# A planner's table of engine times set to other numbers, in a fused four-branch block

## The chip, the core and the metric

The kernel runs on one core of one Trainium2 chip. The metric is the device time of one execution in microseconds (us), as the median over several runs. The core has a matrix engine (TensorE, "PE" in the profile, with "PEld" for its weight loads), a vector engine (VectorE, "DVE"), a scalar engine (ScalarE, "ACT"), GpSimd ("POOL") and SyncE ("SP"). In this kernel SP issues the loads of the weights, POOL most of the branches' own loads and stores, ACT some stores. Each engine works through its own instructions in the order in which they stand in the program.

## The reference

The kernel computes one layer for 256 tokens of 2048 features in float32. Cut to what matters:

```
h = rmsnorm(x, norm_pre)
q, f, i, z_a, u, z_b, rkvwa, z_c, xbc, dt, z_d, gate_pre = h @ w_in   # 2048 x 21648
o_a = hgrn2(q, f, i) * silu(z_a)       # gated linear attention, chunks of 64
o_b = s5(u, ...) * silu(z_b)           # diagonal complex state space model, GLU
o_c = rwkv7(rkvwa, ...) * silu(z_c)    # delta rule, 16 heads of 64
o_d = mamba2(xbc, dt, z_d)             # SSD, 16 heads of 64
merged = sum_b sigmoid(gate_pre[b] + gate_bias[b]) * (o_b @ w_up[b])
out = x + rmsnorm(merged @ w_out, norm_post)
```

## The kernel before

All weights are used once, so the program is one long stream of 444 weight chunks. Each chunk (512 KB) is loaded on SP into `raw` (three buffers), split on ACT into `hi` (a copy in the reduced float32r format, L207) and on DVE into `lo = raw - hi` (L216), and multiplied on PE in three products with a likewise split left side: `pg<-h,hi` twice and `pg<-h,lo` once (L261). `hi` and `lo` have four buffers, so the split of chunk n + 3 is written into the program beside the products of chunk n. In the first part of the stream a chunk is 24 products of 256 columns, later 12 of 512 columns. `pg` is the accumulator of the stream (two buffers in PSUM), `pb` the bank that branch products and transposes use (four banks). `ev` and `evm` are evacuations of `pg`, with a token shift or a convolution.

The branches are generators. Each `yield` ends a stage, a small group of instructions on any engines. The stages are put in between the chunks by `_Stream.run_jobs`: after each chunk it goes through the jobs in order of priority and emits a stage, as long as neither DVE nor ACT is more than `AHEAD` = 3.7 us ahead of PE, where a stage may run only if the job's time stamp lies at most `SLACK` = 1.0 us after PE. These times are no measured times: they are a running estimate, `K.t_pe`, `K.t_dve`, `K.t_act` and so on. Every helper that emits an instruction (`mm`, `tr`, `act`, `tt`, `stt`, `ts`, `ld`, ...) first books its cost with `book` (or `book_dma` for a transfer: 2.0 us and the bytes at 220 KB per us). The estimate is only used to choose the place of each stage in each engine's instruction list.

The branches' names that come up below are these.

- S5 (branch b): its output matrices are loaded (`cn`), masked (`cx`), transposed (`pb<-ident,cx`), evacuated as `cT` and `cng`, and stored; the imaginary part goes through the same tiles after the real one. It then runs in eight tiles of two halves each: loads `us`, `bs`, `cu` on POOL (1.3 MB a tile), products `pb<-us,bs`, four scans into `tb` on DVE, products of `ta` and `tb` with `cu`, and `cu` updated on DVE (two instructions).
- Mamba-2 (branch d): loads `mx`, `mbc`, `dk` on POOL, in two halves; `mrow` holds rows of its step sizes, transposed by `pb<-ident,mrow`.
- RWKV-7 (branch c): sigmoids `sw`, `ic` and squares `sq` on ACT, head sums `pb<-sq,ind`, a store `dinv<-row` and its broadcast load `bc`, scans `cs`, row products `bc`, `k`, Gram blocks `GB` and `L` with masks by POOL's selects, an inverse by back substitution in `XT`, whose result goes through DRAM (`dtt`, `dtn`) into `T` and `TT`, and products `pb<-T,GB`.

Of the kernel before, what the change touches and what calls it, by code (L numbers as in the profile page):

```python
# [60 lines left out]
PE_GAP = 0.0  # L61
# [5 lines left out]
# the functions that each activation table serves  # L67
# [6 lines left out]
class _Kern:  # L74
    """Pools, constants and instruction helpers shared by the weight stream and the branches."""

    def __init__(self, ctx, tc, drams):
# [20 lines left out]
        self.soft = False  # L98
        self.o = {}
# [12 lines left out]
    @staticmethod  # L112
    def live(tiles):
        """How many of the tiles are still referred to; the others are dropped from the list."""
        for i in range(len(tiles) - 1, -1, -1):
            if sys.getrefcount(tiles[i]) <= 2:
                del tiles[i]
        return len(tiles)
# [4 lines left out]
    def wait(self, n):  # L123
        """Until n more slots are free."""
# [5 lines left out]
    def wait_banks(self, n):  # L130
        """Until n more PSUM banks are free."""
# [5 lines left out]
    def fm(self, name, n=2):  # L137
        """A feature-major [128, 4 n, 256] array, in tiles of four feature tiles."""
        return [self.big([128, 4, 256], name=f"{name}{j}") for j in range(n)]
# [22 lines left out]
    def book(self, engine, cost, out, ins):  # L162
        """Book an instruction: it starts when the engine is free and its operands are there."""
# [31 lines left out]
    def act(self, out, in_, func, **kw):  # L195
# [7 lines left out]
        ins = [in_] + [x for x in (kw.get("scale"), kw.get("bias")) if hasattr(x, "tensor")]  # L203
        self.book("t_act", cost, out, ins)
# [4 lines left out]
    def _dve(self, out, ins, ns):  # L209
        """Book a vector instruction; one that reads the last one's output waits for it."""  # L210
        self.book("t_dve", 0.06 + ns * 1e-3, out, ins)
# [15 lines left out]
    def stt(self, out, in0, scalar, in1, op0, op1, **kw):  # L227
        self._dve(out, (in0, in1), self._n(out) * 1.045)
        return self.nc.vector.scalar_tensor_tensor(out=out, in0=in0, scalar=scalar, in1=in1, op0=op0, op1=op1, **kw)  # L229

    def ts(self, out, in0, s1, s2, op0, op1=None):
        self._dve(out, (in0,), self._n(out) * 0.53)
# [21 lines left out]
    def mm(self, out, lhsT, rhs, start=True, stop=True, **kw):  # L254
        n = self._n(rhs)
        if rhs.dtype == F32R:
            cost = n * 0.427e-3 if n >= 256 else n * 1.67e-3
        else:
            cost = max(n * 1.67e-3 * min(out.shape[0], 128) / 128, 0.027)
        self.book("t_pe", cost + PE_GAP * (1 if rhs.dtype == F32R else 2), out, (lhsT, rhs))  # L260
        return self.nc.tensor.matmul(out, lhsT, rhs, start=start, stop=stop, **kw)  # L261

    def tr(self, out, in_, b=0):
        """out = in_ transposed; in_ starts at partition b."""
# [12 lines left out]
    def ld(self, out, in_):  # L277
        """A transfer whose source may still be under way."""
# [3 lines left out]
    def ldx(self, out, in_):  # L282
        """A load of what has long been in DRAM."""
# [5 lines left out]
    def st(self, out, in_):  # L289
        """A store of what the scalar engine has just written."""  # L290
# [11 lines left out]
    def split(self, hi, lo, src):  # L302
        """src (float32 in SBUF) as the exact sum of two float32r parts."""
# [3 lines left out]
    def rstd(self, out, ss, n, eps):  # L307
        """out = 1 / sqrt(ss / n + eps), small tiles."""
# [5 lines left out]
def setup_consts(K):  # L314
    nc = K.nc
    d = K.d
# [22 lines left out]
    # ind[:, g, :] sums each half of the partitions into rows 2 g and 2 g + 1 of 32  # L339
# [15 lines left out]
    # lmask[s, level, t]: s and t (mod 64) are paired at that level of the binary split; level 0 is the diagonal  # L355
# [26 lines left out]
def head_sum(K, ps, i, sq):  # L382
    """Sums over each head's features of tile i, to rows 32 (i % 4) + 2 (i // 4) + half of ps."""
# [4 lines left out]
def bcast_heads(K, dst, src):  # L388
    """src DRAM [4, 4, 256] to dst (two tiles [128, 4, 256]): row (q, 2 g + e) on the 64 partitions of half e."""
# [5 lines left out]
# ---------------------------------------------------------------- RWKV-7  # L395
def rwkv_branch(K, rw):
    """rw: r, k, v (two tiles [128, 4, 256]) and wda [128, 256], after the token shift. Leaves K.o['c']."""
# [94 lines left out]
    # L1[c][e]: on the 64 key partitions of head parity e, rows (a | r) scaled by the decay;  # L492
    # on the other 64 partitions the masked products of k with them
# [37 lines left out]
    for c in range(4):  # L531
# [34 lines left out]
        # token-major copies of the scaled keys  # L566
# [261 lines left out]
def hgrn_half(K, g, load):  # L828
# [42 lines left out]
    k = f  # L871
# [1417 lines left out]
```

## Time and profile before

| what | value |
|---|---|
| median of 3 runs | 1427.38 us (1424.73 to 1429.43) |
| profiled execution, its span | 1427.8 us |
| PE busy | 1390.9 us, 97% |
| DVE busy | 1038.0 us, 73% |
| ACT busy | 827.1 us, 58% |
| POOL busy | 162.0 us, 11% |
| bytes moved | 288.62 MB, mean 202 GB/s |
| chain that ended last | PE 71%, DMA 8%, DVE 8%, issue 6%, ACT 6% |

A time in the profile counts from the start of the span. In a row of the chain stand the start, the duration and the work; in a row of a timeline also, in brackets, the idle time of the engine before it and what ended it. A row of a window shows, for each engine, its busy time and the number of instructions in that window, and at the end the granted clock of TensorE (1.00 is full), the share of the DMA engines that was busy, and GB/s. Buffer numbers are left out of the names there; the lists of instructions below keep them, so `hi43_1895` is the `hi` of chunk 43.

### The profile page before, as it was taken

Reading aid. Unit: us, or ns where it says so; the run is one execution under the profiler, and the core shown is the slowest. Engines: PE = TensorE matmul, PEld = TensorE weight load, DVE = VectorE, ACT = ScalarE, POOL = GpSimd, SP = SyncE. Lnnn points to the kernel's source line nnn. Section 1 sums busy time; section 2 is a strip of 40 time slices with the busy share of each in tenths; the row PEclk is TensorE's granted clock in tenths of the full one; section 3 lists DMA queues with packets and bytes.
Section 4 is the critical chain, followed back from the end, with each engine's and each line's share of the span. In section 5 each row is a group of like instructions: output and inputs, shape, how many; then the busy total and the mean of one; then the engine's idle time right before and its main releaser. Section 6 shows DMA issues by size and latency. Waiting matters only on the chain.

```text
span 1427.8 us, 24645 instructions
## 1 busy us (share of the span) xinstructions
PE 1390.9 (97%) x9751; PEld 1223.2 (86%) x9751; DVE 1038.0 (73%) x1422; ACT 827.1 (58%) x1136; POOL 162.0 (11%) x268
## 2 busy tenths in 40 slices
PE   8999989989999999999999999999999999999997
PEld 7999989989989887888789888888789987888886
DVE  6787488778786784576787699767978788576655
ACT  5455445845456546765578765787556444544442
POOL 6232310010025320011100001000010000000000
PEclk9999999999999999999999999999999999999999
DMA  7878985487657876477876567655686856676664
GB/s 214 239 240 263 279 270 163 135 191 232 206 155 175 228 236 179 142 203 201 232 207 198 181 207 197 211 177 172 193 197 194 214 177 191 213 267 194 183 195 135
DMA packets 199040, 288.62 MB, mean 202 GB/s; under 512 B 12453, under 2 KB 116750, under 8 KB 198926
## 3 DMA queue, kind: packets, MB, share of 16 engines
q1 hardware_dynamic: 169614, 237.15, 54.2%
q0 software_dynamic: 25216, 43.05, 13.9%
q10 hardware_dynamic: 4096, 6.86, 1.4%
q8 instruction: 76, 1.25, 0.3%
q14 instruction: 38, 0.31, 0.1%
HBM read 268.33 MB, written 18.66 MB: 201 GB/s over the span
## 4 chain that ended last, share of the span: by engine, by line
PE 71%; DMA 8%; DVE 8%; issue 6%; ACT 6%; POOL 0%; SPq 0%; ACTq 0%; DVEq 0%; POOLq 0%
PE pg L261 63%; PE pb L261 6%; DMA raw<-in_w_in_dram 6%; DVE lo L216 4%; ACT hi L207 2%; PE pb L267 1%; DVE ta L216 1%; ACT L207 1%; DMA cn<-in_s_c_im_dram 1%; DMA x<-in_x_dram 1%; DVE invtmp L216 0%; ACT hT L207 0%; DVE tb L243 0%; DVE tb L216 0%; DMA ds5b<-bl 0%
## 5 line engine op out<-in xcount | busy, mean ns | idle before, releaser
L216 DVE TENSOR_TENSOR lo<-raw,hi 128x1024 fp32r<-128x1024 f32 x444 | 541.1, 1223 | 350.6 <-ACT hi L207 342.3
L207 ACT ACTIVATE hi<-raw 128x1024 fp32r<-128x1024 f32 x444 | 465.9, 1055 | 532.7 <-PE pg L261 249.1
L261 PE MATMUL pg<-h,hi 128*128 128x256 f32 x2624 | 480.8, 286 | 4.1 <-DVE ev L229 3.6
L261 PE MATMUL pg<-hi,h 128*128 128x512 f32 x1408 | 448.1, 393 | 0.1
L261 PEld LDWEIGHTS pg<-h,hi 128*128 128x128 f32 x2624 | 409.9, 192 | 10.7 <-issue 6.9
L261 PE MATMUL pg<-h,lo 128*128 128x256 f32 x1312 | 371.6, 285 | 5.0 <-DVE lo L216 4.1
L261 PEld LDWEIGHTS pg<-hi,h 128*128 128x128 f32 x1408 | 264.9, 188 | 58.5 <-issue 2.5
L261 PE MATMUL pg<-lo,h 128*128 128x512 f32 x704 | 275.5, 391 | 2.6 <-DVE lo L216 2.4
L261 PEld LDWEIGHTS pg<-h,lo 128*128 128x128 f32 x1312 | 251.0, 192 | 6.7 <-DVE lo L216 5.4
L261 PE MATMUL pg<-hi,o 128*128 128x512 f32 x512 | 164.2, 394 | 0.0
L261 PEld LDWEIGHTS pg<-lo,h 128*128 128x128 f32 x704 | 132.6, 188 | 30.5 <-DVE lo L216 4.5
L261 PEld LDWEIGHTS pg<-hi,o 128*128 128x128 f32 x512 | 96.1, 188 | 21.9 <-issue 1.6
L261 PE MATMUL pg<-lo,o 128*128 128x512 f32 x256 | 99.8, 390 | 0.0
L261 PE MATMUL pg<-hi,mhl 128*128 128x512 f32 x224 | 71.1, 391 | 0.0
L280 POOL DMA_DIRECT2D gb<-in_gate_bias_dram x16 | 8.7, 545 | 541.1 <-DVE gate L216 477.9
L207 ACT ACT_TABLE_LOAD x51 | 65.4, 1283 | 5.3 <-DVE mss L235 2.8
L261 PEld LDWEIGHTS pg<-lo,o 128*128 128x128 f32 x256 | 48.1, 188 | 9.5
L261 PEld LDWEIGHTS pg<-hi,mhl 128*128 128x128 f32 x224 | 42.1, 188 | 8.7
L261 PE MATMUL pg<-lo,mhl 128*128 128x512 f32 x112 | 43.6, 389 | 0.0
L243 DVE TENSOR_TENSOR_SCAN tb<-s5p,ta 128x256 f32<-128x256 f32 x64 | 41.7, 701 | 0.1
L261 PEld LDWEIGHTS pg<-lo,mhl 128*128 128x128 f32 x112 | 21.0, 188 | 4.2
L261 PE MATMUL pg<-ghl,hi 128*128 128x256 f32 x128 | 23.1, 283 | 0.0
(371 smaller groups left out, 1362.6 us busy)
## 6 DMA issues: line engine op xcount, KB each, us to landing
raw<-in_w_in_dram SPq DMA_DIRECT2D x340, 512.0 KB
raw<-in_w_up_dram SPq DMA_DIRECT2D x64, 512.0 KB
raw<-in_w_out_dram SPq DMA_DIRECT2D x32, 512.0 KB
us<-duhl POOLq DMA_DIRECT2D x16, 256.0 KB, 6.4
bs<-ds5b POOLq DMA_DIRECT2D x16, 256.0 KB, 7.6
gb<-in_gate_bias_dram POOLq DMA_DIRECT2D x16, 256.0 KB, 4.7
raw<-in_s_w_glu_dram SPq DMA_DIRECT2D x8, 512.0 KB
x<-in_x_dram SPq DMA_DIRECT2D x4, 512.0 KB
```

The lines of the kernel that those rows point to most:

```text
L207: return self.nc.scalar.activation(out=out, in_=in_, func=func, **kw)
L216: return self.nc.vector.tensor_tensor(out=out, in0=in0, in1=in1, op=op)
L243: return self.nc.vector.tensor_tensor_scan(out=out, data0=data0, data1=data1, initial=0.0, op0=ALU.mult, op1=ALU.add)
L261: return self.nc.tensor.matmul(out, lhsT, rhs, start=start, stop=stop, **kw)
L267: return self.nc.tensor.transpose(out, in_, self.ident[b:b + p, b:b + p])
L280: return self.nc.gpsimd.dma_start(out=out, in_=in_)
```

## The change

The costs that the helpers book are set to other numbers. `PE_GAP` (it was 0) goes. A float32r matmul with 256 columns or more is booked with `n * 0.417e-3 + 0.0133` us in place of `n * 0.427e-3`, and 0.15 us are added whenever matmuls change between the full 128 by 128 array and a part of it. On ACT, 0.09 us are added for each scale or bias that is read from a tile, on DVE 0.065 us for each such scalar of `stt` and `ts`. The other lines of the diff drop comments and docstrings, so that line numbers of the changed kernel are 3 to 9 higher.

```diff
-PE_GAP = 0.0
+POINTER_ACT = 0.09
+POINTER_DVE = 0.065
...
         self.last = None
         self.soft = False
+        self.parted = False
...
         ins = [in_] + [x for x in (kw.get("scale"), kw.get("bias")) if hasattr(x, "tensor")]
+        cost += POINTER_ACT * (len(ins) - 1)
         self.book("t_act", cost, out, ins)
...
-    def _dve(self, out, ins, ns):
-        self.book("t_dve", 0.06 + ns * 1e-3, out, ins)
+    def _dve(self, out, ins, ns, scalars=()):
+        ptr = sum(hasattr(x, "tensor") for x in scalars)
+        self.book("t_dve", 0.06 + ns * 1e-3 + POINTER_DVE * ptr, out, ins)
...
     def stt(self, out, in0, scalar, in1, op0, op1, **kw):
-        self._dve(out, (in0, in1), self._n(out) * 1.045)
+        self._dve(out, (in0, in1), self._n(out) * 1.045, (scalar,))
...
     def ts(self, out, in0, s1, s2, op0, op1=None):
-        self._dve(out, (in0,), self._n(out) * 0.53)
+        self._dve(out, (in0,), self._n(out) * 0.53, (s1, s2))
...
     def mm(self, out, lhsT, rhs, start=True, stop=True, **kw):
         n = self._n(rhs)
         if rhs.dtype == F32R:
-            cost = n * 0.427e-3 if n >= 256 else n * 1.67e-3
+            cost = n * 0.417e-3 + 0.0133 if n >= 256 else n * 1.67e-3
         else:
             cost = max(n * 1.67e-3 * min(out.shape[0], 128) / 128, 0.027)
-        self.book("t_pe", cost + PE_GAP * (1 if rhs.dtype == F32R else 2), out, (lhsT, rhs))
+        parted = out.shape[0] < 128 or lhsT.shape[0] < 128
+        if parted != self.parted:
+            self.parted = parted
+            cost += 0.15
+        self.book("t_pe", cost, out, (lhsT, rhs))
```

The instructions of PE, DVE, POOL and SP stay the same in number; ACT gets four more loads of its function tables (66 in place of 62), because functions of different tables now alternate more often. Some 1800 of PE's 8736 instructions stand elsewhere relative to the others. Three places follow.

The first is ACT where S5's output matrices are evacuated. Before, the transposes stand on PE after the products of chunk 39, and the second ones, for the imaginary part, after chunk 44:

```order
L207 ACTIVATE hi42_1854<-raw42_1786 128x1024
L207 ACTIVATE hi43_1895<-raw43_1818 128x1024
L207 ACTIVATE ev_80_1845<-ev_80_1845 128x512
L292 DMA dbc_96<-ev_80_1845 128x512
L207 ACTIVATE cT_81_1884<-pb_82_1885 128x512
L207 ACTIVATE cT_81_1884<-pb_83_1890 128x512
L207 ACTIVATE cng_84_1930<-pb_82_1885 128x512
L207 ACTIVATE cng_84_1930<-pb_83_1890 128x512
```

In the changed kernel the first transposes stand after chunk 35 and the second ones after chunk 39:

```order
L210 ACTIVATE hi38_1711<-raw38_1645 128x1024
L210 ACT_TABLE_LOAD
L210 ACTIVATE mrow_61_1151<-mrow_61_1151 16x128 x2
L210 ACTIVATE hi39_1754<-raw39_1675 128x1024
L210 ACT_TABLE_LOAD
L210 ACTIVATE ev_76_1702<-ev_76_1702 128x512
L301 DMA dx_95<-ev_76_1702 128x512
L210 ACTIVATE cT_77_1743<-pb_78_1744 128x512
L210 ACTIVATE cT_77_1743<-pb_79_1749 128x512
L210 ACTIVATE cng_82_1797<-pb_78_1744 128x512
L210 ACTIVATE cng_82_1797<-pb_79_1749 128x512
```

Mamba's `mrow` and two table loads stand between the split of chunk 38 and `cT` now, and four chunks lie between the two sets of transposes instead of five.

The second place is POOL's list of loads around Mamba's second half and S5's tile 1. Before:

```order
L280 DMA mx_138_2968<-dx_95 128x1024
L280 DMA mbc_139_2969<-dbc_96 128x512 x2
L280 DMA dk0_143_3010<-dacs_1482 128x8x128
L280 DMA dk1_144_3012<-dacs_1482 128x8x128
L280 DMA lw_157_3258<-in_rwkv_w2_dram 64x1024
L280 DMA lw_157_3258<-in_rwkv_a2_dram 64x1024
L280 DMA bc0_185_3631<-dinv_3626 64x4x256 x2
L280 DMA bc1_186_3632<-dinv_3626 64x4x256 x2
L280 DMA us_188_3708<-duhl_101 64x4x256
L280 DMA bs_189_3709<-ds5b_973 64x8x128
```

In the changed kernel:

```order
L289 DMA mx_141_2960<-dx_95 128x1024
L289 DMA mbc_142_2961<-dbc_96 128x512 x2
L289 DMA us_143_2967<-duhl_101 64x4x256
L289 DMA bs_144_2968<-ds5b_938 64x8x128
L289 DMA us_143_2967<-duhl_101 64x4x256
L289 DMA bs_144_2968<-ds5b_938 64x8x128
L289 DMA cu_145_2973<-ds5c_1215 128x384
L289 DMA cu_145_2973<-du_100 128x256
L289 DMA dk0_147_3007<-dacs_1637 128x8x128
L289 DMA dk1_148_3009<-dacs_1637 128x8x128
L289 DMA lw_159_3136<-in_rwkv_w2_dram 64x1024
L289 DMA lw_159_3136<-in_rwkv_a2_dram 64x1024
```

The six loads of S5's tile 1 (`us`, `bs` twice each, `cu` twice) have moved from behind `bc` to between `mbc` and `dk`.

The third place is DVE ahead of the first products with `T`. Before, these stand on PE after the products of chunk 157:

```order
L216 TENSOR_TENSOR lo157_6213<-raw157_6178,hi157_6212 128x1024
L216 TENSOR_TENSOR lo158_6231<-raw158_6197,hi158_6230 128x1024
L216 TENSOR_TENSOR lo159_6258<-raw159_6216,hi159_6257 128x1024
L229 SCALAR_TENSOR_TENSOR cu_272_5519<-cu_272_5519,pt_115,pb_298_6248 64x256
L216 TENSOR_TENSOR cu_272_5519<-cu_272_5519,pb_298_6248 64x256
L216 TENSOR_TENSOR lo160_6281<-raw160_6234,hi160_6280 128x1024
```

In the changed kernel they stand after chunk 152, so that the splits of 152 to 155 are the last ones ahead of them:

```order
L609 COPY invtmp_293_5683<-XT_292_5682 128x1024
L220 TENSOR_TENSOR lo148_6096<-raw148_6033,hi148_6095 128x1024
L233 SCALAR_TENSOR_TENSOR cu_252_5129<-cu_252_5129,pt_115,pb_298_5784 64x256
L220 TENSOR_TENSOR cu_252_5129<-cu_252_5129,pb_298_5784 64x256
L220 TENSOR_TENSOR lo149_6116<-raw149_6059,hi149_6115 128x1024
L220 TENSOR_TENSOR lo150_6134<-raw150_6099,hi150_6133 128x1024
L220 TENSOR_TENSOR lo151_6163<-raw151_6119,hi151_6162 128x1024
L220 TENSOR_TENSOR lo152_6185<-raw152_6137,hi152_6184 128x1024
L220 TENSOR_TENSOR lo153_6203<-raw153_6166,hi153_6202 128x1024
L220 TENSOR_TENSOR lo154_6221<-raw154_6188,hi154_6220 128x1024
L220 TENSOR_TENSOR lo155_6239<-raw155_6206,hi155_6238 128x1024
```

Before, the update of `cu` stands directly behind the split of chunk 159, at the products with `T`; now it stands behind the split of chunk 148, seven splits ahead of the last one shown.

## The prediction

> **What bounds the kernel now.** I read the page first, then the waits of TensorE, then windows of 50 us, then the chain of waits around each gap.
>
> ```profile
> span 1427.8 us, 24645 instructions
> ...
> PE 1390.9 (97%) x9751; PEld 1223.2 (86%) x9751; DVE 1038.0 (73%) x1422; ACT 827.1 (58%) x1136; POOL 162.0 (11%) x268
> ...
> L216 DVE TENSOR_TENSOR lo<-raw,hi 128x1024 fp32r<-128x1024 f32 x444 | 541.1, 1223 | 350.6 <-ACT hi L207 342.3
> ...
> L207 ACT ACT_TABLE_LOAD x51 | 65.4, 1283 | 5.3 <-DVE mss L235 2.8
> ```
>
> TensorE is busy in 97% of the span, and idle 1427.8 − 1390.9 = 36.9 us, head and tail included. No instruction is dropped, so nothing can be won outside that idle time and the slow clock behind it. The profiled execution (1427.8 us) lies at the median of the runs (1427.38), so the sum is made against 1427.4. The windows show where TensorE loses time (PE busy first, then clock, DMA share, GB/s at the end):
>
> ```profile
> 150.00:200.00 50.00, 44.32 (x346) 43.98 (x345) 31.20 (x48) 21.41 (x29) 11.80 (x18) 0.93 1.08 294
> 400.00:450.00 50.00, 46.98 (x429) 42.26 (x429) 37.53 (x40) 33.41 (x50) 16.64 (x14) 0.97 0.50 143
> 750.00:800.00 50.00, 50.00 (x347) 45.88 (x347) 34.23 (x42) 42.06 (x51) 0.00 (x0) 1.00 0.59 187
> ```
>
> From 750 us on a window is full. What this change can win lies in the first half, where four branches run beside the stream. The waits of TensorE name them (us in total, times, longest):
>
> ```profile
> PE pg L261 <- DVE lo L216: 6.5, 8, 2.2
> ...
> PE pg L261 <- DVE ev L229: 3.6, 1, 3.6
> PE pb L261 <- DVE cu L216: 2.7, 1, 2.7
> PE pb L261 <- DVE tb L216: 2.6, 2, 2.4
> ...
> PE pb L267 <- DVE cx L235: 2.1, 1, 2.1
> ```
>
> The five longest gaps end at 157.4 (cx), 184.2 (ev), 314.4 (lo), 419.7 (tb) and 542.6 us (cu). Each costs more than itself, since the granted clock (third number from the right) is halved behind it:
>
> ```profile
> 157.20:160.70 3.50, 3.34 (x16) 3.37 (x17) 2.47 (x3) 2.56 (x5) 0.00 (x0) 0.51 0.58 166
> 180.00:184.50 4.50, 0.88 (x7) 0.70 (x7) 3.96 (x9) 2.66 (x5) 0.00 (x0) 1.00 1.02 315
> 184.50:188.00 3.50, 3.50 (x19) 3.50 (x18) 1.83 (x3) 3.10 (x6) 0.00 (x0) 0.51 1.03 360
> 188.00:191.50 3.50, 3.50 (x31) 3.50 (x31) 3.38 (x7) 0.32 (x2) 0.00 (x0) 1.00 1.03 340
> 314.20:317.70 3.50, 3.25 (x15) 3.25 (x16) 3.50 (x4) 1.18 (x2) 0.00 (x0) 0.51 1.01 315
> 420.00:423.50 3.50, 3.50 (x22) 2.54 (x15) 2.73 (x4) 0.00 (x0) 0.00 (x0) 0.51 0.86 265
> 542.90:546.40 3.50, 3.50 (x61) 2.95 (x54) 2.32 (x2) 1.06 (x1) 1.04 (x2) 0.51 0.82 241
> ```
>
> After each gap of 2.1 us or more stand some 3.5 us at 0.51 of the clock, then 1.00 again: half of 3.5 us is lost, 1.7 us per gap. The Trainium skill ("TensorE: Matmul & The Clock Gate", section HAM oscillation) warns only of idle gaps above about 3.4 us. By that rule just the 3.6-us gap would bring a slow stretch, and the three other gaps that I take as gone would each be worth 1.7 us less, 5 us in all. This trace does not agree: gaps of 2.1, 2.2, 2.4 and 2.7 us were followed by the half clock too, and the measurement decides.
>
> **What the change does.** It sets only estimates. The chain of waits holds the paces that they should match, with the pieces that the next steps need:
>
> ```profile
> 147.79 8.52 DMA cn<-in_s_c_im_dram
> ...
> 168.57 10.76 DMA raw<-in_w_in_dram
> ...
> 199.43 17.26 PE pg L261 x144
> ...
> 310.41 2.85 DVE bc L229 x7
> ...
> 530.16 9.03 DMA raw<-in_w_in_dram
> ...
> 824.34 16.35 PE pg L261 x72
> ```
>
> 256-wide products take 17.26 / 144 = 0.120 us and 512-wide ones 16.35 / 72 = 0.227 us. Before, the estimate had 0.109 and 0.219; now it has 0.120 and 0.227. A chunk of 24 256-wide products grows in the estimate from 2.62 to 2.88 us. The planner so believes TensorE to be later, and the tests (engines not over 3.7 us ahead of TensorE, a stage's stamp not over 1.0 us ahead) let branch stages in earlier. The dearer pointer operands pull the other way on ACT and DVE, but less. In the order S5 comes forward most: 5 chunks early at its first tile, some 40 at the second half of tile 1, and 12 to 16 later on. So the change moves gaps; I cost the five and what is put in their place.
>
> Gap 1, cx (a loss). S5's output matrices are transposed, evacuated as cT and cng, and only then is the imaginary part cn loaded, masked to cx and transposed again.
>
> ```profile
> 142.57 1.06 ACT L207 ACTIVATE hi<-raw 128x1024 fp32r<-128x1024 f32 x1 [1.20 <-DMA raw<-in_w_in_dram]
> 143.53 0.61 ACT L207 ACTIVATE ev<-ev 128x512 f32<-128x512 f32 x1
> ...
> 144.55 1.09 ACT L207 ACTIVATE cT<-pb 128x512 f32<-128x512 f32 x2 [0.40 <-ACT ev L207]
> 145.52 1.09 ACT L207 ACTIVATE cng<-pb 128x512 f32<-128x512 f32 x2
> ...
> 156.33 0.88 DVE L235 TENSOR_SCALAR cx<-cn,s5pm 128x512 f32<-128x512 f32 x2 [2.92 <-DMA cn<-in_s_c_im_dram]
> ...
> L207 ACT ACTIVATE mrow<-mrow x4: 292/408/419, 93.3 to 122.0; 16x256 f32<-16x256 f32 x2, 16x128 f32<-16x128 f32 x2
> ```
>
> Before, five chunks (14.4 us) stood between the two sets of transposes and TensorE still waited 2.1 us. Now there are four, 2.9 us less cover. Ahead of cT on ACT stand now two table loads (2 × 1.28) and two mrow exponentials (2 × up to 0.41): 3.4 us more, of which 1.6 may fall into the idle 1.20 + 0.40 of these rows. The wait becomes 2.1 + 2.9 + 1.8 to 3.4 = 6.8 to 8.4 us, less about 1 for the six mrow transposes that now stand there; I take 7. The half clock behind it is paid already. Loss 5 us; bounds 3 and 7.
>
> Gaps 2 and 3, transfers that crowd the weight stream:
>
> ```profile
> 162.60 0.66 POOL L280 DMA_DIRECT2D us<-duhl  x1
> ...
> 169.76 0.56 POOL L280 DMA_DIRECT2D mx<-dx  x1
> ...
> 295.36 2.50 POOL L280 DMA_DIRECT2D bc<-dinv  x4 [76.27 <-DMA dinv<-row]
> 297.84 0.64 POOL L280 DMA_DIRECT2D us<-duhl  x1
> ```
>
> Before, S5's loads (us, bs, cu, 1.3 MB) go out right ahead of Mamba's mx and the loads behind it, one weight chunk takes 10.76 us, and ev stands behind the late lo. S5's tile 0 now comes five chunks (14 us) earlier, but the loads of tile 1 fall in with Mamba's second half on the same queue, ahead of its dk. I take 3.0 back of 3.6 + 1.7 = 5.3; bounds 0 and 5.3. In gap 3 the bc loads (1 MB) and S5's tile 1 went out back to back, and now bc stands alone: of 2.2 + 1.7 = 3.9 I take 3.4, bounds 1 and 3.9. What is late next is bc itself, now four chunks behind its store.
>
> Gap 4, tb. POOL's selects ran beside S5's scans:
>
> ```profile
> 410.50 1.47 POOL L275 TENSOR_SCALAR_AFFINE_SELECT GB<-GB 64x1024 f32<-64x1024 f32 x1 [54.77 <-ACT GB L207]
> ...
> 409.75 4.25 DVE L243 TENSOR_TENSOR_SCAN tb<-s5p,ta 128x256 f32<-128x256 f32 x4
> ```
>
> Four scans took 4.25 us there and tb came late. This half stands now in chunk 83, far from the selects; another S5 half is near them. Of 2.4 + 1.7 = 4.1 I take 3.4, bounds 0 and 4.1. Gap 5, cu: the vector engine's cu stood behind a lo whose chunk took 9.03 us, and the products with T waited for its bank. Now no cu stands among the last seven lo ahead of the products with T. 2.7 + 1.7 = 4.4 back; bounds 2 and 4.4.
>
> New places. At chunk 82 ACT must pass eight sigmoids and the squares before TensorE sums them:
>
> ```profile
> 276.43 3.39 ACT L207 ACTIVATE sq<-k,pt 128x256 f32<-128x256 f32 x8
> ...
> L243 DVE TENSOR_TENSOR_SCAN cs<-m,sw 128x512 f32<-128x512 bf16 x4 | 4.6, 1204 | 0.0
> ```
>
> Squares 3.4, sigmoids about 3, hi 1.1 in one split, against two chunks (5.8 us): a wait of 0 to 4, I take 2.5. On the vector engine split 83 gets the four cs scans (4.8 us) with r1 and lo on top of S5's halves. Summing the durations of the trace in the new order, its backlog is 8.7 us there and 5 to 7 at splits 86, 90, 96 and 99 (before: never over 5.0). The lead of lo is three chunks, 8.6 us, so it just covers; I take 1.5 for this and other new tight places, bounds 0 and 20 (below). The four table loads that the new order adds (4 × 1.28 = 5.1 us) lie on ACT, busy 58%, and cost nothing beyond the two counted above; exposed they would cost 5.
>
> Sum: gains 3.0 + 3.4 + 3.4 + 4.4 = 14.2, losses 5.0 + 2.5 + 1.5 = 9.0, net −5.2: 1427.4 − 5.2 = **1422 us**.
>
> **Rivals.** (1) Nothing measurable, 1427 (1423.1 to 1431.7). The gaps only change place: the old order had the same planner and five bad places in 540 us, and a new one has as many. Gains 14 against losses 14. For it: the transfers' estimate is untouched, and two of my losses are of its kind. Against: from 750 us on TensorE never waits, so only half of the stream can go wrong. That the estimates move nothing is excluded by the order. (2) Slower, by one mechanism: the vector engine's backlog from chunk 73 to 100. It decides from the point where the backlog passes 8.6 us, for then lo is late at the products. If the scans and bc run only 10% longer, or wait behind ACT's sigmoids, the five peaks each stop TensorE for some 3 us, with 1.7 of half clock: 5 × 4.7 = 23.5 in place of my 4.0, so 1422 + 19.5 = 1441. For it: 8.7 against 8.6. Against: four of the five peaks leave 1.7 us or more. (3) A larger gain: cx no later than before and all of gaps 2 to 5 gone, 5.3 + 3.9 + 4.1 + 4.4 = 17.7, so 1410.
>
> **How the numbers follow.** The forecast gets 0.45, rival 1 0.28, rival 2 0.18, rival 3 0.09. A measurement of this kernel can tell about 0.3% (4.3 us) from none: faster is below 1423.1, slower above 1431.7. The forecast sits near that border, its own range being 1415 to 1429, so it gives 0.33 to faster and the rest mostly to no change; with rival 3 and some of rival 1, faster 0.46; same 0.33; slower 0.21 (rival 2 and the tail of rival 1). The range goes from 1408, rival 3 with a little more, to 1437, most of the way to rival 2.
>
> **What would show it.** The waits of TensorE for cx near 135 to 145 us should be 6 to 8 us with half clock behind; waits for ev, tb and cu of over 2 us should be gone, with 1.00 in the windows where 0.51 stood; a wait of 1 to 4 us for sq should stand at 265 to 285 us. More lo waits from 250 to 330 us mean rival 2. The forecast is wrong if cx is not late, or if the loads of S5's tile 1 make a weight chunk as late as at 168 us.

## The result, and the profile after

The changed kernel takes 1482.0 us (median of 4 runs, 1478.0 to 1492.9) against 1427.4 before (4 runs, 1424.7 to 1429.4): 55 us slower, ratio 1.040 with a 95% interval of 1.036 to 1.044. The forecast was 1422 with a range of 1408 to 1437. It was wrong in sign and in size.

The profiled execution has a span of 1483.1 us. Two lines of the changed kernel's page answer to those of before:

```profile
span 1483.1 us, 24668 instructions
...
PE 1414.3 (95%) x9751; PEld 1236.4 (83%) x9751; DVE 1043.7 (70%) x1422; ACT 832.9 (56%) x1140; POOL 163.1 (11%) x268
```

The span grew by 55.3 us. TensorE is busy 23.4 us longer with the same instructions (1414.3 against 1390.9), and idle for 68.8 in place of 36.9 us, 31.9 more. The other engines do the same work in nearly the same time.

The waits of TensorE in the changed kernel (us in total, times, longest) say what it was idle for:

```profile
PE pg L270 <- DVE lo L220: 8.2, 12, 2.4
PE pg L270 <- ACT hi L210: 7.2, 4, 3.6
PE pb L270 <- DVE ta L220: 5.7, 3, 2.1
PE pb L276 <- DVE xD L220: 4.9, 1, 4.9
PE pb L270 <- DVE tb L220: 4.9, 5, 1.9
PE pb L276 <- DVE cx L239: 4.5, 1, 4.5
PE pb L270 <- DVE E L220: 4.0, 2, 3.5
PE pg L270 <- DVE ev L233: 4.0, 1, 4.0
```

Before, the stream had five gaps over 1.7 us, 12.9 us in sum. Now it has eleven, 33.9 us in sum. They begin at 109 us (hi, 3.6), 123 (lo, 2.4), 154 (cx, 4.5), 197 (ev, 4.0), 251 (ta, 2.1), 465 (tb, 1.9), 493 (ta, 2.1), 562 (TT and Zs, 2.4), 591 (xD, 4.9), 744 (hi, 2.6) and 910 (E, 3.5). Only cx and ev stood among the five of before. Nor do the gaps keep to the first half: two windows of the changed kernel from the part that was full before (299.89 of the 300 us from 900 to 1200) show it.

```profile
900.00:950.00 50.00, 46.50 (x259) 38.22 (x258) 35.91 (x43) 29.21 (x49) 1.60 (x3) 0.93 0.60 198
...
1100.00:1150.00 50.00, 46.21 (x273) 38.32 (x272) 38.97 (x46) 25.32 (x30) 5.28 (x8) 1.00 0.87 218
```

In the second window no single gap is over 1.7 us; 3.8 us go in small ones. Most of the 23.4 us by which TensorE is busy longer are clock. Windows of the changed kernel behind two of the gaps (the gap in the first row of three, the granted clock third from the right):

```profile
109.00:113.00 4.00, 0.38 (x4) 0.17 (x2) 0.02 (x1) 1.11 (x2) 0.00 (x0) 1.00 0.73 235
113.00:116.50 3.50, 3.04 (x12) 2.74 (x13) 3.50 (x7) 3.41 (x7) 0.00 (x0) 0.50 0.34 98
116.50:120.00 3.50, 3.50 (x19) 3.50 (x18) 2.37 (x5) 3.02 (x4) 0.00 (x0) 0.52 0.19 67
...
591.00:596.20 5.20, 0.33 (x12) 0.19 (x8) 2.83 (x6) 3.48 (x6) 0.00 (x0) 0.82 0.32 100
596.20:599.70 3.50, 3.38 (x10) 2.63 (x11) 3.47 (x4) 2.82 (x5) 0.00 (x0) 0.50 0.22 47
599.70:603.20 3.50, 3.50 (x25) 2.17 (x24) 1.68 (x2) 1.65 (x3) 0.00 (x0) 0.80 0.49 158
```

The half clock lasts not 3.5 us here but up to 7. Summing (1 − granted clock) over windows of 1 us, without the head and the tail of the kernel, gives 8.5 us lost to the clock before, in five stretches of some 3.4 us, and 29.0 us now, in eleven stretches, six of them twice as long. All gaps of the stream together, the small ones too, grew from 22.2 to 54.1 us. So the account is 31.9 us more of gaps + 20.5 us more of clock = 52.4 of the 55.3 us. The two overlap a little, since a slow stretch can begin before its gap ends: counted only while TensorE was busy, the clock is 17.7 us, and 5.7 us are left in which TensorE was busy longer at full clock. What these are, no run shows. By place:

| what | us |
|---|---|
| nine large gaps at new places, 25.4, with nine slow stretches behind them, 23.9 | +49.3 |
| gaps under 1.7 us, 9.3 before and 20.2 now | +10.9 |
| the five old places: 12.9 + 8.5 before, of which cx and ev are left with 8.5 + 5.1 | −7.8 |

What makes the new gaps is seen in timelines of the changed kernel (start us, duration, engine, work; in brackets the idle time before it and what ended it). First the stores of S5's input matrices on POOL, the loads around an S5 tile further on, and selects of RWKV-7:

```profile
95.25 2.33 POOL L289 DMA_DIRECT2D ds5b<-bh  x4 [0.44 <-issue]
97.58 2.30 POOL L289 DMA_DIRECT2D ds5b<-bl  x4
99.87 2.30 POOL L289 DMA_DIRECT2D ds5b<-bh  x4
102.30 0.90 POOL L289 DMA_DIRECT2D cn<-in_s_c_re_dram  x1
...
486.72 1.18 POOL L284 TENSOR_SCALAR_AFFINE_SELECT GB<-GB 64x1024 f32<-64x1024 f32 x1
...
731.12 0.72 POOL L289 DMA_DIRECT2D hv<-dv  x1
731.83 0.65 POOL L289 DMA_DIRECT2D us<-duhl  x1
...
894.50 0.58 POOL L289 DMA_DIRECT2D cu<-du  x1
895.05 0.56 POOL L289 DMA_DIRECT2D hf<-df  x1
```

and the splits of the weight chunks on ACT that waited for their load:

```profile
111.89 1.06 ACT L210 ACTIVATE hi<-raw 128x1024 fp32r<-128x1024 f32 x1 [7.67 <-DMA raw<-in_w_in_dram]
...
745.52 1.06 ACT L210 ACTIVATE hi<-raw 128x1024 fp32r<-128x1024 f32 x1 [7.36 <-DMA raw<-in_w_in_dram]
...
906.58 1.06 ACT L210 ACTIVATE hi<-raw 128x1024 fp32r<-128x1024 f32 x1 [7.64 <-DMA raw<-in_w_in_dram]
```

Twelve stores and a load leave POOL between 95 and 103 us, and ACT stands 7.7 us without a weight chunk. Before, the second twelve of these stores stood behind Mamba's `mrow` and left from 113 us on:

```profile
112.88 0.51 POOL L280 DMA_DIRECT2D dacs<-mrow  x1 [21.20 <-DVE mrow L243]
113.39 2.32 POOL L280 DMA_DIRECT2D ds5b<-bh  x4
```

Ahead of the gaps at 744 and 910 us the loads of an S5 tile went out back to back with HGRN-2's (`hf`, `hq`, `hv`), and ACT stood for 7.4 and 7.6 us. Then the vector engine ahead of the gaps at 197 and 493 us:

```profile
190.56 1.29 DVE L220 TENSOR_TENSOR ta<-ta,tb 128x512 f32<-128x512 f32 x2
...
192.91 2.43 DVE L247 TENSOR_TENSOR_SCAN tb<-s5p,ta 128x256 f32<-128x256 f32 x4
...
196.37 1.22 DVE L220 TENSOR_TENSOR ta<-tb,cs 128x1024 f32<-128x1024 f32 x1
197.50 1.22 DVE L220 TENSOR_TENSOR lo<-raw,hi 128x1024 fp32r<-128x1024 f32 x1
198.64 2.42 DVE L233 SCALAR_TENSOR_TENSOR ev<-pg,pt,ev 128x253 f32<-128x253 f32 x6
...
486.21 3.80 DVE L220 TENSOR_TENSOR ta<-ta,tb 128x512 f32<-128x512 f32 x2
```

The evacuation `ev` stands behind an S5 half, and TensorE needs the bank that it frees. At 486 us the two additions that took 1.29 us at 190 us take 3.80, beside POOL's selects. Eight of the eleven large gaps have S5's work in front of them, in one of these ways or as a step of S5 itself that TensorE waits for (109, 154, 197, 251, 465, 493, 744, 910). That is what the rows show. Whether S5's earlier place is the cause of the loss is a matter for the runs.

### The profile page after: what moved, and what is told of

Same layout as the page of the kernel before. It is cut to its first block, busy times and chain, and to the rows that moved or that the text cites. A ratio compares the mean times of both kernels' runs of the same rounds, so it can differ in the third digit from the quotient of the medians.

```text
span 1483.1 us, 24668 instructions
## 1 busy us (share of the span) xinstructions
PE 1414.3 (95%) x9751; PEld 1236.4 (83%) x9751; DVE 1043.7 (70%) x1422; ACT 832.9 (56%) x1140; POOL 163.1 (11%) x268
## 5 line engine op out<-in xcount | busy, mean ns | idle before, releaser
L270 PE MATMUL pg<-h,hi 128*128 128x256 f32 x2624 | 485.9, 288 | 9.7 <-ACT hi L210 4.6
L270 PE MATMUL pg<-hi,h 128*128 128x512 f32 x1408 | 454.6, 398 | 2.6 <-ACT hi L210 2.6
L270 PEld LDWEIGHTS pg<-hi,h 128*128 128x128 f32 x1408 | 269.0, 191 | 63.8 <-ACT hi L210 3.4
L270 PE MATMUL pb<-ta,cu 128*32 128x256 f32 x128 | 19.6, 408 | 5.7 <-DVE ta L220 5.7
```

## The experiments

Each kernel was run once beside a run of the old kernel on the same chip; the loss is the difference of the two. The old kernel's runs in these groups lay between 1423.0 and 1430.9 us, but the four runs of the changed kernel spread over 15 us (1478.0 to 1492.9). A loss from a single run can so be off by some 10 us, and smaller differences between two kernels prove nothing by themselves. "S5" and "others" are the mean places of the stages of S5 and of the other branches against the old order, in weight chunks (minus is earlier). "Last" is the chunk at which S5's last half stands; the GLU, whose products begin at chunk 380, needs all of S5. Gaps and clock are summed as above. They do not add up to the loss: where long gaps run at half clock (e3, e4, e12) both columns count the same time, and in most slow runs TensorE is also busy longer at full clock, by up to 9.6 us (e10).

| kernel | us | loss | S5 | others | last | gaps | clock |
|---|---|---|---|---|---|---|---|
| before | 1427.4 | | 0 | 0 | 369 | 22.2 | 8.5 |
| the whole change | 1482.0 | 54.6 | −24.0 | −4.7 | 342 | 54.1 | 29.0 |
| e1_mm_only | 1480.7 | 49.8 | −25.1 | −6.0 | 357 | 53.3 | 25.6 |
| e2_no_mm | 1440.1 | 9.2 | +14.3 | +4.3 | 378 | 24.3 | 15.4 |
| e3_pointer_only | 1475.2 | 44.2 | +40.9 | +11.1 | 379 | 56.8 | 34.1 |
| e4_ahead_3p8 | 1453.5 | 22.6 | +11.1 | +3.9 | 379 | 40.8 | 20.5 |
| e5_b_slack_0p9 | 1428.8 | 1.6 | +1.1 | −1.3 | 370 | 18.9 | 10.2 |
| e6_a_slack_m2 | 1442.5 | 15.3 | −1.2 | −0.5 | 373 | 26.8 | 17.0 |
| e7_a_slack_m1 | 1467.0 | 39.8 | −25.8 | +1.1 | 338 | 47.9 | 13.6 |
| e8_a_ahead_2p5 | 1458.4 | 31.2 | −5.3 | −5.8 | 358 | 35.9 | 20.4 |
| e9_a_hold | 1463.3 | 34.9 | +0.4 | −7.9 | 369 | 45.0 | 11.9 |
| e10_a_hold_slack0 | 1462.7 | 34.3 | +0.4 | −2.4 | 369 | 40.1 | 13.7 |
| e11_b_s5early2 | 1453.1 | 24.7 | −13.2 | +2.7 | 367 | 37.0 | 18.7 |
| e12_b_prio2 | 1486.4 | 57.9 | −12.2 | +8.0 | 354 | 60.2 | 42.6 |
| e13_b_mm25 | 1456.9 | 31.6 | −17.4 | −0.8 | 359 | 41.2 | 13.7 |
| e14_a_slack_0p9 | 1478.7 | 53.4 | −22.8 | −4.7 | 357 | 52.8 | 23.9 |
| e15_a_ahead_3 | 1480.8 | 55.5 | −7.2 | −7.5 | 358 | 51.3 | 30.7 |
| e16_b_slack_2 | 1440.7 | 15.4 | +9.4 | +5.6 | 371 | 31.0 | 6.8 |
| e17_parted_only | 1449.8 | 26.8 | +5.1 | +3.4 | 379 | 33.0 | 18.7 |
| e18_a_slack_m1p6 | 1455.1 | 32.1 | −3.0 | +2.5 | 370 | 40.5 | 17.1 |

Two theories run through the expectations. By the first, the **place** decides (theories A, C and D in the expectations): the dearer matmul cost lets branch work in earlier, S5 above all, and where it is crowded it stops the stream. By the second, each order is a **draw** (theory B): any change of a number gives another order, the old one is a good one among many, and the new costs as such are not to blame.

### Which part of the change carries the loss

e1: the matmul cost alone, on top of the old kernel's other costs.

```diff
-POINTER_ACT = 0.09
-POINTER_DVE = 0.065
+POINTER_ACT = 0.0
+POINTER_DVE = 0.0
...
         if parted != self.parted:
             self.parted = parted
-            cost += 0.15
```

> Only the dearer matmul cost (256 wide 0.109 to 0.120 us, 512 wide 0.219 to 0.227); no 0.15 for a change of the array, no pointer costs. In its order branch products stand 8.7 chunks earlier on average (after: 7.3 earlier). Theory A (the dearer TensorE estimate pulls stages forward and eats the distance between producers and TensorE): nearly all of the loss, 1470 to 1490 us. Theory B (the old order was a lucky draw, any reshuffle costs): also slow, but anywhere from 1440 to 1490.

e2: the changed kernel with the old matmul cost.

```diff
-            cost = n * 0.417e-3 + 0.0133 if n >= 256 else n * 1.67e-3
+            cost = n * 0.427e-3 if n >= 256 else n * 1.67e-3
```

> The whole change but the matmul cost, which stays the old one. In its order branch products stand 5.6 chunks later than before on average, none earlier. Theory A: no loss, 1420 to 1435 us. Theory B: a loss of its own, 1440 to 1490 us, since 1201 of 1392 branch products stand in another chunk.

Measured: 1480.7 and 1440.1 us. The matmul cost alone brings 49.8 of the 54.6 us and moves S5 as far as the whole change does (−25.1 chunks); without it 9.2 us are lost and S5 stands later than before. The first speaks for the place. The second lies between the two: above what the place allowed (1420 to 1435), and at the lower edge of a draw (1440 to 1490). But the parts do not add up, as e3 shows: only the dearer pointer operands.

```diff
-            cost = n * 0.417e-3 + 0.0133 if n >= 256 else n * 1.67e-3
+            cost = n * 0.427e-3 if n >= 256 else n * 1.67e-3
...
         if parted != self.parted:
             self.parted = parted
-            cost += 0.15
```

> Only the costs of pointer operands on ScalarE and VectorE. Branch products stand 15 chunks later on average. Theory A: no loss, 1420 to 1435 us. Theory B: 1440 to 1490 us.

Measured: 1475.2 us, a loss of 44.2, with S5 41 chunks *later*. The waits of TensorE in e3, and rows of its timeline (products of a branch; in brackets the idle time before):

```profile
PE pb L269 <- DVE ta L220: 17.5, 3, 10.5
PE pb L269 <- issue: 16.8, 2, 15.3
```

```profile
1246.32 1.07 PE L269 MATMUL pb<-ta,cu 128*32 128x256 f32 x4 [3.54 <-DVE ta L220]
...
1266.92 1.07 PE L269 MATMUL pb<-ta,cu 128*32 128x256 f32 x4 [15.35 <-issue]
...
1281.68 1.07 PE L269 MATMUL pb<-ta,cu 128*32 128x256 f32 x4 [10.47 <-DVE ta L220]
...
1284.70 0.80 PE L269 MATMUL pg<-ghl,hi 128*128 128x256 f32 x2
```

From 1242.8 to 1284.7 us not one weight product runs. The GLU's first chunk needs the output of S5, S5 was not through, and the program put all of S5's last tile between two chunks, each of its steps exposed. So lateness has its own wall, at chunk 380 (last half at 379), and it is nearly as dear as the whole change. e17 does the third part alone, the 0.15 us for a change between full and partial array:

```diff
-POINTER_ACT = 0.09
-POINTER_DVE = 0.065
+POINTER_ACT = 0.0
+POINTER_DVE = 0.0
...
-            cost = n * 0.417e-3 + 0.0133 if n >= 256 else n * 1.67e-3
+            cost = n * 0.427e-3 if n >= 256 else n * 1.67e-3
```

> Only the 0.15 us for a change of the array. S5 5.1, the others 3.4 chunks later, but S5's last half stands at the gate (379). Loss only at the end, from 1200 us on, 5 to 25 us as with AHEAD 3.8: 1432 to 1453 us.

Measured: 1449.8, a loss of 26.8. The size was expected, the place was not: S5's last half stands at 379 here too, but the gap at the GLU is only 1.2 us; the clock is down in the first 600 us (0.95 from 150 to 300 and 0.93 from 450 to 600 us), behind gaps at other places (Zs 5.7, ev 3.6 us). The three parts alone cost 50, 44 and 27 us and together 55. They push in both directions, and no part's loss is a share of the whole.

### How much any other order costs

e4 and e5 change a threshold of the old kernel by a tenth and keep its costs.

```diff
-AHEAD = 3.7
+AHEAD = 3.8
```

> The kernel before with AHEAD 3.8 in place of 3.7, all costs the old ones: a change without meaning that still puts 1060 of 1392 branch products into another chunk, 4.9 later on average. Theory A: no loss beyond noise of placement, 1420 to 1440 us. Theory B: 1440 to 1490 us.

```diff
-SLACK = 1.0
+SLACK = 0.9
```

> The kernel before with SLACK 0.9 in place of 1.0. 1020 of 1392 branch products stand in another chunk, but the mean place is 0.9 chunks earlier only, and S5's last half ends at chunk 370 (before 369; the gate that needs it comes at 380). Theory C (two walls: stages placed earlier crowd the first half, stages placed later run into the gate at chunk 380; the old order lies between them): 1424 to 1440 us. Theory B (lucky draw, any reshuffle costs): 1445 to 1485.

Measured: 1453.5 and 1428.8 us. An edit that touches no cost loses 22.6 us in e4, inside the range of the draw, more than half of it at the same wall: S5's last half at chunk 379 and one wait of TensorE at 1245 us,

```profile
PE pb L261 <- DVE ta L216: 15.0, 3, 14.3
```

while e5 is within the measurement of no change. Its waits of TensorE hold the only two gaps over 1.7 us in its stream:

```profile
PE pg L261 <- DVE ev L229: 5.5, 1, 5.5
...
PE pg L261 <- ACT hi L207: 2.1, 1, 2.1
```

Its lost time is that of before (gaps 18.9, clock 10.2, against 22.2 and 8.5), at other places. So an order as good as the old one exists beside it. It is also the nearest of all: its branch products stand 2.0 chunks from their old places on the mean, earlier or later, those of e4 5.4. e16 goes the other way with `SLACK`.

```diff
-SLACK = 1.0
+SLACK = 2.0
```

> The kernel before with SLACK 2.0: S5 9.4, the others 5.6 chunks later, S5's last half at chunk 371, so that it does not run into the gate at 380. If only early crowding and the gate cost: 1424 to 1437 us. If any other draw costs: 1440 to 1470.

Measured: 1440.7, a loss of 15.4 with S5 9 chunks later. No gate is in play (last half at 371), and S5 is not early. That is outside what crowding and the gate alone allowed (1424 to 1437), at the lower edge of a draw.

### Can the thresholds put the new costs right

If the place decides, the changed kernel with thresholds that bring S5 back should be as fast as the old one. e6, e7 and e18 lower `SLACK` in the changed kernel, e8 and e15 `AHEAD`, and e14 changes `SLACK` by a tenth only.

```diff
-SLACK = 1.0
+SLACK = -2.0
```

> All new costs, with SLACK -2.0 in place of 1.0: a stage has to lie 2 us behind TensorE's estimate before the next one is let in. Mean place 0.6 chunks earlier than before, S5's last half at chunk 373. Theory C: 1425 to 1445 us, since the place is the old one, though the costs are the new ones. Theory B: 1445 to 1485.

```diff
-SLACK = 1.0
+SLACK = -1.0
```

> All new costs, with SLACK -1.0. Mean place 2.6 chunks earlier than before, but S5 still early (last half at chunk 338, as in the changed kernel: 342). If the distance between a stage and the next one is what was lost, 1435 to 1455 us; if S5 being early among the other branches is the cause by itself, 1465 to 1485.

```diff
-AHEAD = 3.7
+AHEAD = 2.5
```

> All new costs, with AHEAD 2.5 in place of 3.7: no stage is let in while the estimate of VectorE or ScalarE is over 2.5 us ahead of TensorE's. Mean place 5.7 chunks earlier than before. If the vector engine's backlog is what makes TensorE wait, 1435 to 1455 us; if it is the distance between stages, no gain, 1465 to 1485.

Measured: 1442.5, 1467.0 and 1458.4 us. With −2.0, S5 is back within 1.2 chunks of its old place and 39 of the 55 us are recovered; with −1.0 S5 has not moved (−25.8) and 15 us are; e8 has S5 at −5.3 and stays 31 us behind. e7 lies where S5's early place was to cost by itself (1465 to 1485), and e8 between its two ranges. The order of the three by S5's place is right, and the old time is not reached in any.

```diff
-SLACK = 1.0
+SLACK = 0.9
```

> The changed kernel with SLACK 0.9 in place of 1.0, a change without meaning: S5 -22.8, the others -4.7 chunks, as in the changed kernel (-24.0, -4.7). Place sets the time: 1470 to 1492 us. Draw sets the time: anywhere from 1440 to 1500.

```diff
-AHEAD = 3.7
+AHEAD = 3.0
```

> The changed kernel with AHEAD 3.0: S5 -7.2, the others -7.5 chunks, near the run with AHEAD 2.5 (-5.3, -5.8, 1458 us). Place: 1452 to 1468 us. Draw: 1440 to 1500.

```diff
-SLACK = 1.0
+SLACK = -1.6
```

> All new costs with SLACK -1.6: S5 3.0 chunks earlier, the others 2.5 later, last half at 370. Place: 1428 to 1446 us, like the run with SLACK -2.0 (1442). Draw: anywhere from 1440 to 1490.

Measured: e14 1478.7, e15 1480.8, e18 1455.1. e14 is the counterpart of e5 at the new costs. The order is another in its detail and the time is the changed kernel's within 4 us; e1, with S5 at −25 as well, lies within 2 us of it. But the three are nearly one order: against the changed kernel the branch products stand 0.3 chunks away on the mean in e14 and 1.9 in e1, against the old one 7.8 and 9.4. Their large gaps stand at the same places: `cx` from 144 to 155 us, `ta` from 487 to 493, TT and Zs from 557 to 562, xD from 591 to 596 (the times at which the gaps begin). So they show that this order is slow and stays so, and not that every order with S5 so early is: e7, with S5 at −25.8 and the other branches at +1.1, lies 12 to 15 us lower. And e15 came out above what was expected of it: S5 at −7.2, hardly earlier than in e8, and 22 us slower than e8. Its waits of TensorE show gaps of S5's again (ta 15.3 us in five waits, cx 5.8, bx 4.9, ev 4.1). e18, with S5 at −3.0, loses 32.1 where e6 at −1.2 loses 15.3; its 1455 is above the range set for the place (1428 to 1446). Mean place alone does not order these.

### S5 alone put back, S5 alone moved

e9 takes the changed kernel and holds each of S5's halves until the chunk at which it began in the old order. All costs are the new ones. e10 adds `SLACK = 0.0`, to move the other branches back too.

```diff
+S5_FROM = [49, 63, 89, 121, 131, 175, 188, 208, 223, 261, 275, 306, 320, 332, 347, 361]
...
+        while K.stream.step < S5_FROM[2 * i + hh]:
+            yield 1
...
+        K.stream = self
```

> All new costs, but each of S5's 16 halves is not let in before the chunk at which it began in the old order. S5's products then stand where they stood (mean +0.4 chunks, changed kernel: -24), the other branches' 7.9 chunks earlier (changed kernel: -4.7). Theory D (S5 early among the other branches costs by itself, and so does a shorter distance between the other branches' stages): the S5 part of the loss goes, 1440 to 1460 us. S5 alone: 1425 to 1437. Distance alone: 1470 to 1485.

> As the one before, with SLACK 0.0 in place of 1.0: S5 mean +0.4 chunks, the others 2.4 earlier. Theory D: most of what was left goes too, 1428 to 1445 us. If the distance of the others plays no part, the same as the one before within 5 us.

Measured: 1463.3 and 1462.7 us. S5 stands at +0.4 in both, and a loss of 34 to 35 us remains. Moving S5 back recovers 20 us, not 55 (e9 lies 3 us above its range), and bringing the others from −7.9 to −2.4 recovers nothing. That was a clear miss for e10, for which theory D had 1428 to 1445. The waits of TensorE in e10:

```profile
PE pg L271 <- DVE lo L221: 15.0, 19, 3.0
PE pg L271 <- ACT hi L211: 8.1, 5, 3.2
...
PE pg L271 <- DVE ev L234: 3.1, 1, 3.1
```

Nineteen waits for `lo` and five for `hi`: the stream's own splits come late, in many small pieces, behind other branches' work and late chunks (ACT waits 250.3 us in sum for `raw` from `in_w_in_dram`, 203.8 before). The converse is e11, the old kernel with S5's stages let in 2 us earlier, and e12, with S5 raised in the order of priority.

```diff
-        return job.ready <= self.step and job.stamp <= self.K.t_pe + SLACK
+        return job.ready <= self.step and job.stamp <= self.K.t_pe + SLACK + (2.0 if job.name[:2] == "s5" else 0.0)
```

> The kernel before with the old costs; only for S5's stages SLACK is 3.0 in place of 1.0. S5's products stand 13 chunks earlier in the mean, the others 2.7 later, S5's last half at chunk 367. Theory D: the S5 part of the loss at half its size, 1440 to 1455 us. If S5 early costs nothing: 1424 to 1434.

```diff
-PRIO_S5 = 5
+PRIO_S5 = 2
```

> The kernel before with the old costs; S5's priority is put ahead of HGRN-2's. Nothing changes up to chunk 207; from there S5 comes up to 40 chunks earlier and ends at chunk 354 instead of 369, and HGRN-2 later. If S5 early costs wherever it is: 1440 to 1460 us. If it costs only in the first half, where Mamba-2 and RWKV-7 run beside it: 1424 to 1435.

Measured: e11 1453.1 with S5 at −13.2 and the rest 2.7 later: this order, with S5 let in earlier, costs 24.7 us. That is about what e4, e16 and e17 lose with S5 later (15 to 27), so the run alone does not part the two theories. e12 loses 57.9, far over what was expected, by a cause that was not in it. Its waits of TensorE and rows of its timeline:

```profile
PE pb L261 <- DVE E L216: 22.2, 7, 5.8
PE pb L267 <- DVE oa L216: 9.6, 2, 6.3
```

```profile
1147.04 1.98 PE L261 MATMUL pb<-E 128*64 128x64 f32 x32 [3.26 <-DVE E L216]
...
1188.95 0.80 PE L261 MATMUL pg<-hi,o 128*128 128x512 f32 x1 [0.74 <-ACT o L207]
```

From 1135 to 1189 us no weight product runs. HGRN-2, pushed back by S5, was not done when its up projection was due, and its chain ran exposed, as S5's does in e3. The two walls belong to whichever branch is moved.

e13 takes a quarter of the matmul step, in the old kernel.

```diff
-            cost = n * 0.427e-3 if n >= 256 else n * 1.67e-3
+            cost = n * 0.0004245 + 0.003325 if n >= 256 else n * 1.67e-3
```

> The kernel before with a quarter of the new matmul step (256 wide 0.109 to 0.112 us), nothing else. S5 jumps 17 chunks early in the mean, the others only 0.8. Theory D (S5 early among the other branches costs by itself): 1445 to 1465 us, in the first 600 us. If only the distance between stages counts, which is hardly changed: 1425 to 1437.

Measured: 1456.9, a loss of 31.6 with S5 at −17.4. A quarter of the change in the number makes seven tenths of the shift and six tenths of the loss; the response is not proportional to the number.

### What the runs settle, and what not

Settled: the matmul cost is enough for nearly the whole loss (e1), and it pulls branch work forward. The order that it makes is slow in three kernels that nearly share it (the change, e1, e14: 1479 to 1482). Delaying a branch too far costs as much, at the gate that needs it (e3, e12, in part e4). In all, 19 other orders were run, the change among them. One equals the old order (e5) and none beats it; the losses of the others run from 9 to 58 us. The old order is a favourable one, and nearly every edit tried gave it up.

In part argued: that S5's early place is what makes the order slow. For it: S5 put back recovers 20 us (e9), thresholds that undo the shift recover up to 39 (e6), and S5 let in earlier costs 25 (e11) and 32 (e13). Against it: e16 and e17 lose 15 and 27 us with S5 later and hardly a wait at the gate, and e9 and e10 keep 34 us with S5 in its old place, e10 only 2.9 chunks from the old order on the mean.

Not settled: what makes two orders with the same mean places differ by 15 to 30 us (e6 and e18; e8 and e15; e9 and e10 against before). It should lie in which single stages meet, but no run isolates that. Nor was it tried whether the gaps at 109, 744 and 910 us go if the planner books transfers that share bandwidth. It books each with a fixed 2 us and its bytes, so it sees none of these bursts, before or after. Nobody can say from these runs either whether some threshold makes the new costs faster than the old ones; six were tried.

## Why the prediction was wrong, point by point

- **What bounds the kernel**: right. Nearly all that changed lies in gaps of TensorE and in the half clock, 31.9 + 17.7 of 55.3 us without the overlap of the two.
- **Direction of the shift**: right. Branches come earlier, S5 most, by 24 chunks on the mean. Its size was read too small: the prediction has "12 to 16 later on" behind tile 1, but in the two orders the first products of S5's halves from tile 2 on stand 11 to 49 chunks earlier, and only three of these twelve halves 12 to 16. The second half of tile 2 comes 49 chunks earlier (its first products run at 480.7 us in place of 618.9). The gaps at 465 and 493 us are waits of the two halves of this tile.
- **Gap 1, cx, a wait of 7 us and a loss of 5**: right in kind. The wait is 4.5 us, at 154 us and not at 135 to 145, so it grew by 2.4. The clock behind it was not paid already, since the slow stretch became twice as long: 1.7 us more. The loss of 4.1 is inside the bounds (3 and 7), but only through a term that had been put at nothing.
- **Gap 2, ev, 3.0 us back**: wrong. It waits 4.0 us (3.6 before). TensorE goes on at 201.2 us with `ev`, which stands behind an S5 half on the vector engine. A late weight chunk is still there (ACT stands idle 8.6 us before the split at 203.1 us), but the gap ends before it. The slow stretch behind is as long as before, so 0.4 us were lost and nothing came back; the lower bound, 0, was just missed.
- **Gap 3, lo, 3.4 us back**: right at its place. The 2.2 us are gone, and from 250 to 350 us TensorE waits for `lo` once, 0.3 us.
- **Gap 4, tb, 3.4 us back**: wrong in total. The gap went from 420 us and came back as two, at 465 (1.9) and 493 us (2.1), with slow stretches of 3.4 and 6.8 us: 4.0 + 5.1 = 9.1 us in place of 4.1. The prediction itself said that another S5 half stands near the selects, took 0.7 us off the gain for it, and bounded the gain by 0.
- **Gap 5, cu, 4.4 us back**: right at its place, but the next step behind the products with T (554 us) waits instead, TT and Zs 2.4 us at 562, and xD 4.9 us at 591.
- **Squares at chunk 82, a wait of 2.5**: wrong. There is none; a neighbouring wait for `sw` is 0.2 us.
- **Table loads at nothing**: open. ScalarE is busy 56% of a longer span. One table load (1.28 us, at 593.68) stands in the chain ahead of the xD gap, but the same one stood there before, without a gap. No run tested the four added ones alone.
- **1.7 us of half clock per gap**: too little. It held for the old gaps (8.5 / 5); the new ones cost 29.0 / 11 = 2.6 each.
- **"I take 1.5 for this and other new tight places, bounds 0 and 20"**: this is the step that failed. The large gaps at new places cost 25.4 + 23.9 = 49.3 us, and small ones 10.9 more. With the squares it was priced at 4.0, and even its upper bound of 20 was a third of what came.

The sum counted the five known gaps one by one as chances to win and the unknown ones with one small term. But a shift of S5 by some 24 chunks puts nearly every one of its stages beside other neighbours, and each new meeting is a chance for a gap of the kind that the old profile showed at five places. The old trace could price such a meeting (2 to 4 us and the clock). It could not show how many there would be, and I took the five known ones as if they were all. The two orders could have shown how many stages move and how far, and there the shift of S5's later tiles was read too small. The second half of tile 2 on TensorE, before and in the changed kernel:

```profile
618.94 0.64 PE L261 MATMUL pb<-us,bs 128*128 128x256 f32 x4
...
480.69 0.74 PE L270 MATMUL pb<-us,bs 128*128 128x256 f32 x4
```

The same mistake is in "what this change can win lies in the first half" and in the argument against rival 1 that "only half of the stream can go wrong". True of winning, wrong of losing: the part without gaps before now has those at 744 and 910 us, and from 900 to 1200 us TensorE is now busy 290.8 in place of 299.9 us. Rival 1 (gaps change place) named the mechanism and then assumed that a new order has as many gaps as the old. It has 11 over 1.7 us in place of 5, and e5 has 2. Rival 2 (the vector engine's backlog from chunk 73 to 100) is refuted by the same `lo` waits as gap 3; its time of 1441 was nearer by luck.

What the prediction should have asked is how its end with a loss looks when many places move: ten new gaps at the old price of 2.6 + 1.7 us (12.9 / 5 and 8.5 / 5) are 43 us. With that as a rival, the range would have reached 1460 or more.

## What to carry to other kernels

A planner's costs and its thresholds are one setting: making one cost truer moves everything that the thresholds let through, and in this kernel 17 of the 18 other edits that were run, sensible or not, made it slower, by 9 to 58 us. So run several thresholds along with each new cost, and judge a cost model by the measured times of several orders, not by its truth. When predicting such a change, count the stages that get new neighbours and price each chance with a gap and its clock; do not price only the gaps that the old profile happens to show. And look at both walls: work that is let in early can crowd the stream, and work that is put off runs exposed at the first consumer that needs it.

## What the runs showed of the hardware

**The half clock goes by a fixed grid of 3.41 us, and gaps far shorter than that bring it.** In the stream of each of the 20 profiles of this case all half-clock stretches begin on one grid of 3.413 us (to within 0.01 us; where it lies differs from run to run) and last whole steps of it: one step 79 times, two 44 times, more 14 times, up to 41 us in e3. What TensorE does in one step goes with the clock of the next. Of 109 steps at full clock in which TensorE was busy under 45%, 107 were followed by a half clock; of 45 steps with 45 to 55% it was 10, of 7929 above 55% only 20. So some 1.9 us of idle time inside one step suffice (55% of 3.41), and a gap of that length matters or not by how it lies to the grid. By length, a half clock was there within 4 us of the end of 7 of 37 gaps of 0.95 to 1.2 us, 15 of 56 of 1.2 to 1.7 us, 27 of 38 of 1.7 to 2.1 us, 53 of 62 of 2.1 to 3.5 us, and all 47 over 3.5 us. Once at half clock, the next step stayed slow in 73 of 82 steps with TensorE busy under 90%, and in 20 of 148 above. That goes with the doubled stretches of the changed kernel. The Trainium skill ("TensorE: Matmul & The Clock Gate", section What's actually happening) says that activity is watched over a free-running window of 3413 ns. The grid and the durations agree. Its section HAM oscillation gives the rule of no idle gaps above about 3.4 us; by these counts that is too lax, for two in three gaps of 1.7 to 2.1 us already bring the half clock.

**Two additions on the vector engine took 1.29 us alone and 3.80 beside POOL's selects** (the rows at 190.56 and 486.21 us above). The split `lo` shows the same: in the changed kernel's trace 435 of its 444 instances overlap no select and none of these takes over 1.23 us; beside a select it takes up to 2.18. The Trainium skill ("SBUF — State Buffer", section Who interferes with whom) says that a vector instruction with both inputs in SBUF contends with a GpSimd instruction that reads SBUF. The rows agree.
